# ScalarE seeds two kept PSUM banks with the doubled residual for the plain down products of a macaron decoder

## The chip, the core and the metric

The kernel runs on one core of one Trainium2 chip. The metric is the device time of one execution in microseconds (us). TensorE (PE in the profile, PEld for its weight loads) multiplies, VectorE (DVE) and ScalarE (ACT) do the elementwise work, and SyncE (SP) issues the DMAs. Products are summed in PSUM banks, of which the program uses eight as single tiles of 128 x 512 fp32.

## What is computed

Two layers of a decoder over 512 tokens with 1024 features. Each layer is an FFN half-step, a mixer (gated linear attention in the first, stick-breaking attention in the second) and another FFN half-step; a last RMSNorm follows.

```python
def swiglu(h, w_gate, w_up, w_down):
    return (jax.nn.silu(h @ w_gate) * (h @ w_up)) @ w_down
...
x = x + 0.5 * swiglu(rmsnorm(x, ffn1_norm[i]), ffn1_w_gate[i], ffn1_w_up[i], ffn1_w_down[i])
...
x = x + 0.5 * swiglu(rmsnorm(x, ffn2_norm[i]), ffn2_w_gate[i], ffn2_w_up[i], ffn2_w_down[i])
```

D_FF is 2816, all data are fp32. The change touches the four FFN half-steps only, in the line `x + 0.5 * (...) @ w_down`.

## The kernel before

**Layout.** The residual x stays in SBUF for the whole program as eight tiles `xs[k]` of 128 features x 512 tokens. Weights come from HBM in entries of up to 1 MB.

**A product in three passes.** Each fp32 operand is split into a high half rounded to the matmul's reduced format and a low remainder. For weights, ACT casts the high half (`wh`, L138) and DVE subtracts to get the low one (`wl`, L139); for activations the same is done in `cut` (L806 and L807). A product is then three matmuls, high by high, low by high and high by low (`mm3`, L82, through `mm`, L79; the profile shows these under L80).

**The feed.** The program is a list of entries (`Feed`, `Entry`): a load, a split and a body with the products. A started entry splits up to two entries after it ahead of time, and loads further. Bodies are generators; within an FFN they run one after another. Each engine works its own instruction list in order, and the order of a list comes from a scheduler that places instructions of the five engines by their dependences.

**PSUM banks.** `psum()` hands out one whole bank a call. Without a tag it takes the next letter of `order`, "aazzztto", and so goes through 8 banks in turn: two of tag a, three z, two t, one o. A bank can be written again when the reader of its last tile is done.

**An FFN phase** (class `FFN`, L605, run four times) splits the 11 column chunks of the gate and up weights in the groups `((0, 2), (2, 4), (4, 6), (6, 8), (8, 9), (9, 11))`. For the first chunks, gate and up tiles are plain products (`feat`); for the later ones they go through `seven()`, a Strassen-like scheme of seven half products in place of eight. A `seven` takes the banks `ps_w`, `ps_q` and `ps_z`. Its first product goes to `ps_w`; ACT copies it to `ps_z` (L736), onto which later products add without a fresh start; ACT copies further halves to SBUF (L739, L742, L754), DVE adds (L755, L759), and the gate is a Silu on ACT (L719) for the gate weights or a multiplication by it on DVE (L722) for the up weights. The last gate of an up `seven` reads `ps_w`, which frees it.

**Down.** A group's down products follow while the next group's gate and up run. Groups 1 and 3 use `seven_down` (L353), which opens two `ps_w` banks, copies them to two `ps_z` banks on ACT (L402), opens one `ps_q` (products L384) and adds to x on DVE (L390). Groups 0, 2 and 4 use `down` (L310): groups 0 and 2 have 4 entries of two output tiles, each tile 4 x 3 matmuls of 512 columns; group 4 has 2 entries of four output tiles with 2 x 3 matmuls each. The first two entries of group 0 run just ahead of group 1, and the first of them is given `late=1`: its two tiles are summed over three of four parts first, and then both are finished. After a tile's last product DVE adds half of it to x (L339). Group 5's entries also go through `down`, but with `nxt` set, which starts the next norm with each finished tile; in the last FFN `back_tok` and `to_tokens` do this part instead. The first FFN of the second layer follows the last FFN of the first layer at once.

**Where the FFN phases lie** in the trace: about 60 to 320, 607 to 862, 930 to 1190 and 1492 to 1747 us, called the first to the fourth FFN below. Outside of these lie the mixers, the norms and the transitions.

Of the kernel before, what the change touches and what calls it, by code (L numbers as in the profile page):

```python
# [14 lines left out]
AF = mybir.ActivationFunctionType  # L15
ALU = mybir.AluOpType
# [14 lines left out]
def turns(t):  # L31

    return t.rearrange("p (two n) -> p n two", two=2)


def flat(ps):

    return ps.rearrange("p (n two) -> p two n", two=2)


def pair(t):

    return t.rearrange("p (two n) -> p two n", two=2)
# [3 lines left out]
def decoder(ctx: ExitStack, tc: tile.TileContext, a: dict, out: bass.AP):  # L47
    nc = tc.nc
# [6 lines left out]
    sp = ctx.enter_context(tc.tile_pool(name="sp", bufs=1))  # L55
    pp = ctx.enter_context(tc.tile_pool(name="pp", bufs=1, space=PSUM))
    banks = {"a": 2, "z": 3, "t": 2, "o": 1}
    order = "aazzztto"
    turn_ = [0]

    def psum(name, tag=None):
        if tag is None:
            tag = order[turn_[0] % 8]
            turn_[0] += 1
        return pp.tile([P, T], F32, tag=tag, bufs=banks[tag], name=name)

# [9 lines left out]

    xs = [xp.tile([P, T], F32, name=f"x{k}") for k in range(KD)]

    def mm(ps, l, r, first, last):  # L79
        st["pe"] = nc.tensor.matmul(ps, l, r, start=first, stop=last).ins  # L80

    def mm3(ps, wh, wl, mh, ml, first, last):  # L82
        mm(ps, wh, turns(mh), first, False)
        mm(ps, wl, turns(mh), False, False)
        mm(ps, wh, turns(ml), False, last)

# [108 lines left out]
    def feat(ch, f, evac, tag=None, defer=None):  # L197


        def body(W):  # L200
            (wh, wl), = W
            ps = psum("ps_f", tag)
            for part in (range(u, u + KD // 4) for u in range(0, KD, KD // 4)):
                for k in part:
                    mm3(ps, wh[:, k], wl[:, k], st["h"][k], st["l"][k], k == 0, k == KD - 1)
                if part[-1] == KD - 1:
                    if defer is None:
                        evac(ps)
                    else:
                        defer.append((evac, ps))  # L210
                yield

        feed.q.append(Entry([(ch, lambda t: t[:, :, f * P : (f + 1) * P], KD, P)], body))
        feed.q[-1].evac = evac
# [29 lines left out]
    def back(w, r0, nf, hs, scale, nxt, late=0, tags=(None,) * 8):  # L244


        for dh in range(2):
# [18 lines left out]
            def acc(m, dh=dh, accs=accs):  # L266
                if m == len(accs):
                    accs.append(psum("ps_b", tags[dh * 4 + m]))
                return accs[m]

            def prod(W, u, kk, m, f, acc=acc):
                wh, wl = W[u]
                s = slice(m * P, (m + 1) * P)
                mm3(acc(m), wh[:, kk, s], wl[:, kk, s], hs[f][0], hs[f][1], f == 0, f == nf - 1)
# [37 lines left out]
    def down(w, r0, nf, hs, part, nxt, late=0):  # L312


        nd = KD // nf
        src = w[r0 : r0 + nf * P, part * nd * P : (part + 1) * nd * P]
        ch = Chunk(src.rearrange("(f p) c -> p f c", p=P), nf, nd * P)
        ch.few = True

        def body(W):  # L320
            (wh, wl), = W
            acc = []

            def prod(m, fs):
                if m == len(acc):
                    acc.append(psum("ps_d"))
                s = slice(m * P, (m + 1) * P)
                for f in fs:
                    mm3(acc[m], wh[:, f, s], wl[:, f, s], hs[f][0], hs[f][1], f == 0, f == nf - 1)

            if late:
                for m in range(nd):
                    prod(m, range(nf - late))
            for m in range(nd):
                prod(m, range(nf - late if late else 0, nf))
                ps = acc[m]
                k = part * nd + m
                x = pair(xs[k])
                nc.vector.scalar_tensor_tensor(  # L339
                    out=x, in0=flat(ps), scalar=0.5, in1=x, op0=ALU.mult, op1=ALU.add  # L340
                )
                if nxt is not None:
                    nxt(k)
                yield

        feed.q.append(Entry([(ch, lambda t: t, nf, nd * P)], body))

    def seven_down(pool, w, r0, hs, part):
# [128 lines left out]
    st = {}  # L477
# [76 lines left out]
    def sums_wide(pool):  # L554

        ss = st["ss"]
        h = sp.tile([P, T], F32R, tag="sq", name="sh")
        nc.scalar.copy(h, ss)
        l = pool.tile([P, T], F32R, tag="t", name="sl")
        nc.vector.tensor_tensor(out=l, in0=ss, in1=h.bitcast(F32), op=ALU.subtract)  # L560
        st["wide"] = ps = psum("ps_R")
        mm(ps, ones_r, turns(h), True, False)
        mm(ps, ones_r, turns(l), False, True)

    def rstd_wide():

        ps = st["wide"]
        v = sp.tile([P, T], F32, tag="ss", name="v")
        nc.vector.tensor_scalar(
            out=pair(v), in0=flat(ps), scalar1=1.0 / D, scalar2=EPS, op0=ALU.mult, op1=ALU.add  # L570
        )
        y = st["R"] = sp.tile([P, T], F32, tag="sq", name="R")
        act(y, v, AF.Ln)
        act(y, y, AF.Exp, scale=-0.5)
        nc.scalar.activation(ps, y, AF.Square)
        nc.vector.scalar_tensor_tensor(out=v, in0=ps, scalar=-0.5, in1=v, op0=ALU.mult, op1=ALU.mult)
        nc.vector.scalar_tensor_tensor(out=y, in0=v, scalar=1.5, in1=y, op0=ALU.add, op1=ALU.mult)

    def two_halves(between=None):

        feed.finish()
        g = [feed.start(), feed.start()]
        for i in range(3):
            for x in g:
                next(x, None), next(x, None)
            if i == 0 and between is not None:
                between()

    def new_norm():
        st["h"], st["l"] = st["nh"], st["nl"]  # L590

    def flush(deferred):
        for evac, ps in deferred:
            evac(ps)
        deferred.clear()

    def exp_ln_tables(after):
        with tc.issue_after(after):
            st["tab"] = nc.scalar.preload_act_table_set("natural_log_exp_and_others").ins
# [7 lines left out]
    class FFN:  # L607
# [294 lines left out]
        def run(self, between=None):  # L902
            with tc.tile_pool(name="hp", bufs=8, reuse_waits="tile") as self.hp, tc.tile_pool(
                name="tp", bufs=5, reuse_waits="tile"
            ) as self.tp:
                st["few"] = self.hp
                new_norm()
                if st["ss"] is not None:
                    if self.after_ffn:
                        exp_ln_tables(st["closed"])  # L910
                    two_halves(lambda: sums_wide(self.tp))
                    rstd_wide()
                flush(self.defer)
                def spread(todo, n):
                    for i in range(n):
                        for piece in todo[i * len(todo) // n : (i + 1) * len(todo) // n]:
                            piece()
                        feed.entries(1)

                spread(self.normed_input(), self.NORMED - 2)  # L920
                self.normed = True
                st["h"], st["l"] = zip(*self.n)
                todo = self.sums()
                spread(todo[:5], self.sums_by - self.NORMED)
                feed.entries(1, True)
                for piece in todo[5:]:
                    piece()
                feed.entries(self.count - self.sums_by - 1, True)
                if between is not None:
                    with tc.issue_after(st["closed"]):  # L930
                        nc.scalar.preload_act_table_set("sqrt_and_others")
                    feed.q[feed.pos].split()
                    between(self.tp)
                feed.entries(self.total - self.count)


    class GLA:
# [968 lines left out]
```

## Time and profile before

| what | value |
| --- | --- |
| runs, us | 1781.41, 1781.2, 1780.84 (median 1781.2) |
| the profiled execution, us | 1780.26 |
| its span from first to last instruction, us | 1778.3 |
| granted TensorE clock, mean | 1.00 |
| DMA moved | 179.24 MB, mean 101 GB/s |

The profile is one execution. A group's row gives its busy time, the mean of one instruction in ns, and the idle time of its engine ahead of it with the releaser. A timeline row begins with start and duration in us and names line, operation and tiles (out<-in); "x2" joins two of a kind. In brackets stands the idle time before it and the instruction that ended it. PE's matmuls overlap: a row lasts longer than the distance to the next. A row of the chain of waits gives the start, the time spent and the engine, tile, line and count.

### The profile page before, as it was taken

The page shows a single profiled execution, that of the slowest core. Times are in us where ns is not written, and L with a number is a line of the kernel's source. Part 1 is how long each engine was busy: PE and PEld are TensorE (multiplying, and loading weights), DVE is VectorE, ACT ScalarE, POOL GpSimd, SP SyncE. Part 2 cuts the span into 40 slices and gives each one's busy share as a digit, 9 for nine tenths or more (in the row PEclk, how much of TensorE's full clock was granted, in tenths as well). Part 3 has the DMA queues.
Part 4 walks back from the last instruction along what each step waited for, and adds up shares of the span by engine and source line. Part 5 has one row for each costly group of instructions (what it writes and reads, how often), then busy time and mean ns, then how long its engine had stood idle before and what let it go on. Part 6 is the DMA issues. An engine that isn't in the chain of part 4 may idle for free.

```text
span 1778.3 us, 31182 instructions
## 1 busy us (share of the span) xinstructions
PE 1760.1 (99%) x12714; PEld 1631.7 (92%) x12714; DVE 1538.5 (87%) x2527; ACT 1050.5 (59%) x1830; POOL 9.8 (1%) x24
## 2 busy tenths in 40 slices
PE   9999999999999999999999999999999999999998
PEld 8999999889888899999889999999888888999997
DVE  8999798786878999889798988977898679998986
ACT  7556455554655556555555555655888755565554
POOL 0000000100000000000000000000000000000000
PEclk9999999999999999999999999999999999999999
DMA  5433334322122333333333333322212233333331
GB/s 167 142 115 112 107 96 132 93 71 72 49 95 95 104 110 119 107 107 108 109 93 119 96 119 103 124 84 83 83 48 72 71 95 119 110 105 111 105 126 52
DMA packets 178755, 179.24 MB, mean 101 GB/s; under 512 B 4082, under 2 KB 170276, under 8 KB 178612
## 3 DMA queue, kind: packets, MB, share of 16 engines
q1 hardware_dynamic: 177760, 175.91, 31.6%
q8 instruction: 99, 1.62, 0.4%
q0 software_dynamic: 608, 1.05, 0.2%
q14 instruction: 44, 0.36, 0.1%
q10 hardware_dynamic: 244, 0.29, 0.0%
HBM read 175.17 MB, written 2.10 MB: 100 GB/s over the span
## 4 chain that ended last, share of the span: by engine, by line
PE 64%; DVE 25%; ACT 7%; issue 3%; DMA 1%; SPq 0%; DVEq 0%; ACTq 0%
PE ps_w L709 14%; PE ps_d L80 12%; PE ps_f L80 8%; DVE wl L139 7%; PE ps_q L709 7%; PE ps_t L80 5%; PE ps_z L709 3%; PE ps_b L80 3%; ACT wh L138 3%; PE ps_w L384 2%; DVE x L390 2%; DVE ts L816 1%; PE ps_q L384 1%; PE ps_z L1394 1%; DVE xn L800 1%
## 5 line engine op out<-in xcount | busy, mean ns | idle before, releaser
L139 DVE TENSOR_TENSOR wl<-raw,wh 128x1024 fp32r<-128x1024 f32 x241 | 254.9, 1058 | 58.1 <-ACT wh L138 57.5
L138 ACT CAST wh<-raw 128x1024 fp32r<-128x1024 f32 x241 | 221.6, 920 | 72.4 <-PE ps_f L80 21.5
L139 DVE TENSOR_TENSOR wl<-s,wh 128x1024 fp32r<-128x1024 f32 x176 | 214.2, 1217 | 42.2 <-ACT wh L138 41.9
L138 ACT CAST wh<-s 128x1024 fp32r<-128x1024 f32 x176 | 184.2, 1047 | 102.9 <-DVE s L701 25.7
L709 PE MATMUL ps_w<-th,wh 128*128 128x256 f32 x864 | 239.8, 278 | 3.7 <-ACT ps_z L736 2.7
L709 PE MATMUL ps_w<-th,wl 128*128 128x256 f32 x864 | 237.6, 275 | 0.0
L709 PE MATMUL ps_w<-tl,wh 128*128 128x256 f32 x864 | 237.6, 275 | 0.0
L709 PEld LDWEIGHTS ps_w<-th,wh 128*128 128x128 f32 x864 | 165.8, 192 | 7.4 <-ACT ps_z L736 7.1
L80 PE MATMUL ps_f<-xh,wh 128*128 128x512 f32 x432 | 166.8, 387 | 0.9 <-DVE x L260 0.9
L709 PEld LDWEIGHTS ps_w<-tl,wh 128*128 128x128 f32 x864 | 165.9, 192 | 0.0
L709 PEld LDWEIGHTS ps_w<-th,wl 128*128 128x128 f32 x864 | 165.8, 192 | 0.0
L80 PE MATMUL ps_f<-xh,wl 128*128 128x512 f32 x432 | 164.2, 380 | 0.5 <-DVE wl L139 0.5
L80 PE MATMUL ps_f<-xl,wh 128*128 128x512 f32 x432 | 164.0, 380 | 0.0
L80 PE MATMUL ps_d<-hl,wh 128*128 128x512 f32 x416 | 158.0, 380 | 0.9 <-DVE hl L807 0.8
L80 PE MATMUL ps_d<-hh,wh 128*128 128x512 f32 x416 | 157.7, 379 | 0.2 <-ACT hh L806 0.2
L80 PE MATMUL ps_d<-hh,wl 128*128 128x512 f32 x416 | 157.7, 379 | 0.0
L138 ACT CAST wh<-rawd 128x1024 fp32r<-128x1024 f32 (+1 forms) x100 | 82.9, 845 | 60.1 <-PE ps_d L80 45.2
L139 DVE TENSOR_TENSOR wl<-rawd,wh 128x1024 fp32r<-128x1024 f32 (+1 forms) x100 | 95.7, 961 | 14.7 <-ACT wh L138 14.7
L80 PEld LDWEIGHTS ps_f<-xh,wh 128*128 128x128 f32 x432 | 81.7, 189 | 12.1 <-DVE x L260 1.3
L80 PEld LDWEIGHTS ps_f<-xl,wh 128*128 128x128 f32 x432 | 81.7, 189 | 11.5
L80 PEld LDWEIGHTS ps_f<-xh,wl 128*128 128x128 f32 x432 | 81.7, 189 | 11.1 <-DVE wl L139 0.9
L339 DVE SCALAR_TENSOR_TENSOR x<-ps_d,x 128x512 f32<-128x512 f32 x120 | 79.8, 682 | 13.8 <-PE ps_d L80 13.7
(352 smaller groups left out, 5247.9 us busy)
## 6 DMA issues: line engine op xcount, KB each, us to landing
raw<-in_ffn_w_gate_dram SPq DMA_DIRECT2D x43, 1024.0 KB, 5.4
raw<-in_ffn_w_up_dram SPq DMA_DIRECT2D x43, 1024.0 KB, 5.3
rawd<-in_ffn_w_down_dram SPq DMA_DIRECT2D x84, 512.0 KB, 3.6
raw<-in_gla_w_in_dram SPq DMA_DIRECT2D x12, 1024.0 KB, 5.3
raw<-in_sb_w_in_dram SPq DMA_DIRECT2D x16, 512.0 KB, 3.7
raw<-in_gla_w_out_dram SPq DMA_DIRECT2D x4, 1024.0 KB, 5.2
raw<-in_sb_w_in_dram SPq DMA_DIRECT2D x4, 1024.0 KB, 5.0
raw<-in_sb_w_out_dram SPq DMA_DIRECT2D x4, 1024.0 KB, 5.1
```

Source lines behind the costliest of these rows:

```text
L80: st["pe"] = nc.tensor.matmul(ps, l, r, start=first, stop=last).ins
L138: st["cut"] = nc.scalar.copy(h[:, k], part).ins
L139: nc.vector.tensor_tensor(out=l[:, k], in0=part, in1=h[:, k].bitcast(F32), op=ALU.subtract)
L339: nc.vector.scalar_tensor_tensor(out=x, in0=flat(ps), scalar=0.5, in1=x, op0=ALU.mult, op1=ALU.add)
L384: st["pe"] = nc.tensor.matmul(ps, l_, r_, start=first and c + n == 0, stop=c == 1 and n == 2, skip_group_check=True).ins
L390: nc.vector.scalar_tensor_tensor(out=x, in0=ps, scalar=0.5, in1=x, op0=ALU.mult, op1=ALU.add)
L709: st["pe"] = nc.tensor.matmul(o, l_, r_, start=first and j + n == 0, stop=j == 3 and n == 2, skip_group_check=True).ins
L800: nc.vector.scalar_tensor_tensor(out=t, in0=xs[k], scalar=g, in1=st["R"], op0=ALU.mult, op1=ALU.mult)
L816: nc.vector.tensor_tensor(out=o, in0=p, in1=q, op=ALU.subtract)
L1394: nc.tensor.matmul(o_, l_, r_, start=first, stop=last, skip_group_check=True)
```

## The change

In an FFN phase the turn of banks becomes "aazzzo", six banks, and the two of tag t are kept for `down`. In every plain `down` entry without `nxt` (groups 0, 2 and 4, ten entries in each FFN) the first two tiles go to these two banks. The first two such tiles of each FFN are summed and added as before. For each later one, ACT writes 2x into the bank (new line L329 of the changed kernel), all products add to it without a fresh start, and ACT writes half of the bank back to x (L349) in place of DVE's half-add (now L351). In the entries with four tiles (group 4) the third and fourth tile stay as they were. After the phase the turn of eight banks comes back. Products, their order and the DMAs stay the same.

```diff
@@ -55,12 +55,12 @@
     sp = ctx.enter_context(tc.tile_pool(name="sp", bufs=1))
     pp = ctx.enter_context(tc.tile_pool(name="pp", bufs=1, space=PSUM))
     banks = {"a": 2, "z": 3, "t": 2, "o": 1}
-    order = "aazzztto"
+    order = ["aazzztto"]
     turn_ = [0]
 
     def psum(name, tag=None):
         if tag is None:
-            tag = order[turn_[0] % 8]
+            tag = order[0][turn_[0] % len(order[0])]
             turn_[0] += 1
         return pp.tile([P, T], F32, tag=tag, bufs=banks[tag], name=name)
 
@@ -76,13 +76,13 @@
 
     xs = [xp.tile([P, T], F32, name=f"x{k}") for k in range(KD)]
 
-    def mm(ps, l, r, first, last):
-        st["pe"] = nc.tensor.matmul(ps, l, r, start=first, stop=last).ins
-
-    def mm3(ps, wh, wl, mh, ml, first, last):
-        mm(ps, wh, turns(mh), first, False)
-        mm(ps, wl, turns(mh), False, False)
-        mm(ps, wh, turns(ml), False, last)
+    def mm(ps, l, r, first, last, onto=False):
+        st["pe"] = nc.tensor.matmul(ps, l, r, start=first, stop=last, skip_group_check=onto).ins
+
+    def mm3(ps, wh, wl, mh, ml, first, last, onto=False):
+        mm(ps, wh, turns(mh), first, False, onto)
+        mm(ps, wl, turns(mh), False, False, onto)
+        mm(ps, wh, turns(ml), False, last, onto)
 
 
 
@@ -319,14 +319,23 @@
 
         def body(W):
             (wh, wl), = W
-            acc = []
+            acc, seeded = [], []
+            if nxt is None:
+                for m in range(2):
+                    acc.append(psum("ps_s", "t"))
+                    seeded.append(st["seeds"] > 1)
+                    st["seeds"] += 1
+                    if seeded[m]:
+                        nc.scalar.activation(flat(acc[m]), pair(xs[part * nd + m]), AF.Copy, scale=2.0)
 
             def prod(m, fs):
                 if m == len(acc):
                     acc.append(psum("ps_d"))
+                    seeded.append(False)
                 s = slice(m * P, (m + 1) * P)
                 for f in fs:
-                    mm3(acc[m], wh[:, f, s], wl[:, f, s], hs[f][0], hs[f][1], f == 0, f == nf - 1)
+                    first, last = f == 0 and not seeded[m], f == nf - 1
+                    mm3(acc[m], wh[:, f, s], wl[:, f, s], hs[f][0], hs[f][1], first, last, seeded[m])
 
             if late:
                 for m in range(nd):
@@ -336,9 +345,12 @@
                 ps = acc[m]
                 k = part * nd + m
                 x = pair(xs[k])
-                nc.vector.scalar_tensor_tensor(
-                    out=x, in0=flat(ps), scalar=0.5, in1=x, op0=ALU.mult, op1=ALU.add
-                )
+                if seeded[m]:
+                    nc.scalar.activation(x, flat(ps), AF.Copy, scale=0.5)
+                else:
+                    nc.vector.scalar_tensor_tensor(
+                        out=x, in0=flat(ps), scalar=0.5, in1=x, op0=ALU.mult, op1=ALU.add
+                    )
                 if nxt is not None:
                     nxt(k)
                 yield
@@ -904,6 +916,7 @@
                 name="tp", bufs=5, reuse_waits="tile"
             ) as self.tp:
                 st["few"] = self.hp
+                order[0], st["seeds"] = "aazzzo", 0
                 new_norm()
                 if st["ss"] is not None:
                     if self.after_ffn:
@@ -932,6 +945,7 @@
                     feed.q[feed.pos].split()
                     between(self.tp)
                 feed.entries(self.total - self.count)
+                order[0] = "aazzztto"
 
 
     class GLA:
```

## The prediction

> **What bounds the kernel now.** I read the page's busy times first, then its chain, then the stretches of the four FFN phases, since only those run under the change.
>
> ```profile
> span 1778.3 us, 31182 instructions
> PE 1760.1 (99%) x12714; PEld 1631.7 (92%) x12714; DVE 1538.5 (87%) x2527; ACT 1050.5 (59%) x1830; POOL 9.8 (1%) x24
> PE 64%; DVE 25%; ACT 7%; issue 3%; DMA 1%; SPq 0%; DVEq 0%; ACTq 0%
> ```
>
> PE works 99% of the span. The chain gives DVE 25%, but a chain follows the event that came last by the profile and can run along a DVE stretch while PE works too. So the stretches decide (span, then busy us and count of PE, PEld, DVE, ACT, POOL, clock, DMA share, GB/s):
>
> ```profile
> 60.00:320.00 260.00, 259.23 (x2084) 251.29 (x2083) 234.72 (x382) 145.00 (x255) 7.77 (x15) 1.00 0.36 112
> 930.00:1190.00 260.00, 258.28 (x2080) 250.81 (x2080) 233.89 (x380) 143.82 (x253) 0.53 (x1) 1.00 0.34 106
> ```
>
> PE lacks 0.8 of 260 us in the first FFN and 1.7 in the third, at full clock and a DMA share of 0.36. PE is the bound; DVE, at 90%, is close behind. The waits of the weight loads (total, times, longest) show what a faster DVE or ACT could give back:
>
> ```profile
> PEld ps_w L709 <- ACT ps_z L736: 7.1, 18, 1.4
> PEld ps_w L384 <- DVE x L390: 1.3, 6, 0.3
> ```
>
> That is 8.4 us in 24 waits. After a wait the next matmul also starts late: the one that waited lasts 0.38 instead of 0.28 (rows at 949.58 and 948.12 below), so 0.10 more each, 10.8 us in all. This is the ceiling for a gain.
>
> The steady pitch, from the chain: 24 down products in 5.18 us, that is 2.59 a tile, and 12 of the seven-product kind in 1.34.
>
> ```profile
> 93.30 5.18 PE ps_d L80 x24
> 98.48 1.34 PE ps_w L709 x12
> ```
>
> **Removed and added work.** The removed instruction is DVE's half-add; ACT's seed and writeback have no row of their own, so I take ACT's nearest ones into and out of a bank.
>
> ```profile
> L339 DVE SCALAR_TENSOR_TENSOR x<-ps_d,x 128x512 f32<-128x512 f32 x120 | 79.8, 682 | 13.8 <-PE ps_d L80 13.7
> L1584 ACT ACTIVATE ps_bt<-x 128x512 f32<-128x512 f32 x7 | 4.2, 602 | 7.9 <-DVE x L1574 7.9
> L1567 ACT COPY x<-ps_T 128x512 f32<-128x512 f32 x8 | 4.0, 624 | 0.3 <-PE ps_T L1562 0.3
> ```
>
> Each FFN has 10 plain entries with two such tiles, of which the first two are not seeded: 4 x 18 = 72. DVE loses 72 x 0.682 = 49 us (87% to about 83%), ACT gains 72 x (0.602 + 0.624) = 88 us (59% to about 64%). PE's products and SP's DMAs are the same in number and order. So nothing follows from busy time: only what makes PE wait, or stop waiting, counts.
>
> **Term 1, the first seeded pair of each FFN: +8.2.** The first entry fills the two kept banks unseeded, and DVE empties them with the old half-add. The second entry follows directly on PE. Before, it took two fresh banks; now its first product waits for that half-add and then for a seed. DVE reaches the half-add late, behind splits. Per FFN: PE's first product of the second entry, DVE's half-adds, and for two of them what stands ahead on DVE.
>
> ```profile
> 58.98 0.38 PE L80 MATMUL ps_d<-hh,wh 128*128 128x512 f32 x1
> 58.78 1.22 DVE L139 TENSOR_TENSOR wl<-raw,wh 128x1024 fp32r<-128x1024 f32 x1
> 59.91 1.28 DVE L339 SCALAR_TENSOR_TENSOR x<-ps_d,x 128x512 f32<-128x512 f32 x2
> 606.39 0.38 PE L80 MATMUL ps_d<-hh,wh 128*128 128x512 f32 x1
> 606.42 1.28 DVE L339 SCALAR_TENSOR_TENSOR x<-ps_d,x 128x512 f32<-128x512 f32 x2
> 930.99 0.38 PE L80 MATMUL ps_d<-hh,wh 128*128 128x512 f32 x1
> 931.03 1.28 DVE L807 TENSOR_TENSOR tl<-ts,th 128x512 fp32r<-128x512 f32 x2
> 932.24 0.68 DVE L339 SCALAR_TENSOR_TENSOR x<-ps_d,x 128x512 f32<-128x512 f32 x1
> 1491.40 0.38 PE L80 MATMUL ps_d<-hh,wh 128*128 128x512 f32 x1
> 1491.50 1.28 DVE L339 SCALAR_TENSOR_TENSOR x<-ps_d,x 128x512 f32<-128x512 f32 x2
> ```
>
> The first half-add of each pair ends 0.68 after it starts; a handover takes about 0.04 (a product chain ends at 99.82, ACT's copy starts at 99.86, below) and ACT to PE about 0.06 (a copy ends at 949.52, PE starts at 949.58, below); the seed takes 0.60. So PE starts 1.38 us after DVE's half-add does: 61.29, 607.80, 933.62, 1492.88, which is 2.3 + 1.4 + 2.6 + 1.5 = 7.8 us late, with 4 x 0.10 for the slow restart 8.2. The change leaves DVE's order ahead of these half-adds as it was and takes nothing off DVE there. The second seed is not late: its product comes a tile of 2.59 later. Bounds: 2.9 if DVE were on time and only the seed and the restart counted (4 x 0.72); 10.6 if each seed stood one more ACT operation of 0.6 back. I take the worked value. Behind the waiting seed ACT has the second seed, then the writeback, which waits for PE itself, and then a cast that waited 7.55 us for DVE:
>
> ```profile
> 65.49 1.07 ACT L138 CAST wh<-s 128x1024 fp32r<-128x1024 f32 x1 [7.55 <-DVE s L701]
> ```
>
> So in the first FFN nobody else is held up; the cast can slip with PE. Every later seed has time: its bank is written back after the entry before, and between the two stand products of a seven (the entry that ends at 98.48 is followed by one), several times the seed's 0.60, so it costs PE nothing while ACT is not behind.
>
> **Term 2, six banks in turn: +2.7, small reuses +0.4.** Under eight banks the product of `seven_down` that opens `ps_q` found a long free bank. Under six it gets the bank of the preceding seven's `ps_w`, which DVE's gate L722 frees. I compared each reuse six allocations back with the row that frees it; three come out late by more than the handover:
>
> ```profile
> 1121.63 0.28 PE L384 MATMUL ps_q<-hh,wh 128*128 128x256 f32 x1
> 1119.15 1.05 ACT L138 CAST wh<-s 128x1024 fp32r<-128x1024 f32 x1 [0.91 <-PE ps_q L709]
> 1120.72 1.22 DVE L139 TENSOR_TENSOR wl<-s,wh 128x1024 fp32r<-128x1024 f32 x1
> 1122.46 0.41 DVE L722 TENSOR_TENSOR o<-ps_w,o 128x256 f32<-128x256 f32 x1
> 680.22 0.28 PE L384 MATMUL ps_q<-hh,wh 128*128 128x256 f32 x1
> 681.03 0.42 DVE L722 TENSOR_TENSOR o<-ps_w,o 128x256 f32<-128x256 f32 x1
> 824.68 0.28 PE L384 MATMUL ps_q<-hh,wh 128*128 128x256 f32 x1
> 825.12 0.42 DVE L722 TENSOR_TENSOR o<-ps_w,o 128x256 f32<-128x256 f32 x1
> ```
>
> The gates end at 1122.87, 681.45 and 825.54: 1.24 + 1.23 + 0.86 = 3.3 us late, the upper end. With DVE relieved the split ahead could start when its cast ends (1119.15 + 1.05 + 0.04 = 1120.24 instead of 1120.72), so 0.48 comes off, 0.76 remains, and for three 2.3, the lower end. I take 2.4, nearer the relieved case because DVE does lose work, and 0.3 for restarts. Reuses that come out within a few tenths (copies into `ps_z`, the last transposes) I put at 0.4, between 0 and one more gate of 1.3.
>
> **Term 3, ACT's queue: +0.5.** A writeback waits at the head of ACT's queue for the end of its tile, and behind it stand a cast, a seed and the `ps_z` copy on which the next seven depends.
>
> ```profile
> 98.52 1.07 ACT L138 CAST wh<-rawd 128x1024 fp32r<-128x1024 f32 x1 [2.55 <-PE ps_d L80]
> 99.86 0.36 ACT L736 COPY ps_z<-ps_w 128x256 f32<-128x256 f32 x1 [0.26 <-PE ps_w L709]
> ```
>
> Here the down tile ends at 98.48. Writeback to 99.14, cast to 100.2, seed to 100.8, less some 0.09 of overlap at each boundary (the DVE rows at 58.78 and 59.91 overlap so), copy to about 100.95. PE needs it when the `ps_q` products end, 99.82 + 1.34 = 101.16. So it is hidden by 0.2. There are about a dozen such passages: nothing if each keeps its 0.2, 2.6 if each misses by 0.2. I take 0.5.
>
> **Term 4, waits that go: -4.4.** Three waits close behind the FFN starts come from ACT and DVE running late there; a PE set back by term 1 no longer meets them.
>
> ```profile
> 948.12 0.28 PE L709 MATMUL ps_q<-tl,wh 128*128 128x256 f32 x1
> 949.15 0.37 ACT L736 COPY ps_z<-ps_w 128x256 f32<-128x256 f32 x1
> 949.58 0.38 PE L709 MATMUL ps_w<-th,wh 128*128 128x256 f32 x1 [1.19 <-ACT ps_z L736]
> 76.95 0.38 PE L709 MATMUL ps_w<-th,wh 128*128 128x256 f32 x1 [0.16 <-ACT ps_z L736]
> 1499.68 0.38 PE L709 MATMUL ps_w<-th,wh 128*128 128x256 f32 x1 [0.26 <-ACT ps_z L736]
> ```
>
> The first is 949.58 - 948.12 less the pitch of 0.11, 1.35; the idle shown is 0.16 shorter, so the others are 0.32 and 0.42; with restarts 2.4. Of the other 8.4 of the ceiling I take a quarter, 2.0: DVE's lighter load brings the sums earlier, but the copy itself hangs on ACT, which gets more to do. Bounds 0 and 8.4.
>
> **Sum.** 8.2 + 2.7 + 0.4 + 0.5 - 4.4 = +7.4 on the profiled execution's 1780.26 (span 1778.3 and 2.0 around it): 1787.7. The median of the runs, 1781.2, lies 0.9 above that execution; between the two I say 1788.
>
> **The rivals.** Relief of DVE wins (faster): all 10.8 us of waits go, term 1 falls to its 2.9 and term 2 to 2.3 + 0.3, so 1780.3 - 10.8 + 2.9 + 2.6 = 1775. For it: DVE's 87% and 25% of the chain. Against it: 7.1 of the 8.4 us wait on an ACT copy, and term 1's half-adds are late in a stretch where nothing leaves DVE. It decides once the `ps_z` waits fall below about 1 us and the first seeds cost under 1 us each; chance 0.08. [...]
>
> No change: terms 1 to 3 come, but the set-back lets DVE and ACT catch up for a whole FFN and all waits go, 11.8 - 10.8 = +1, 1782. For it: the waits are short (7.1 in 18). Against: they recur through the FFN, far from its start. Chance 0.2.
>
> ACT becomes the bound: each of the dozen passages misses by a seed less its slack, 0.4, and 0.1 for the restart, 13 x 0.5 = 6.5 instead of 0.5, 1794. For it: ACT works in order and its queue now has waits on PE in it. Against: ACT at 64%. Chance 0.14.
>
> That the accumulation fails to take up the seed isn't among them: L736 already lets ACT fill a bank to which products add.
>
> **How the numbers follow.** Forecast 0.58, rivals 0.08, 0.2, 0.14. About 0.2% or 3.6 us can be told from no change: below 1777.6 is faster, above 1784.8 slower. The forecast's own range is 1783 to 1792. Faster 0.09, same 0.21 (the second rival and the forecast's low edge), slower 0.70. The range 1781 to 1795 leaves out the first rival and the ends.
>
> **What would show it.** The waits should list four on ACT's seeds, 1.3 to 2.6 us each, 7.8 together, and three of some 0.8 of `seven_down`'s `ps_q` on DVE's gate; `ps_z` waits should fall from 7.1 to 3 or 4. DVE near 1490 us busy, ACT near 1138. Wrong if the seeds wait under 1 us each, or if `ps_z` waits grow past 9.

## The result and the profile after

The changed kernel takes 1791.84 us (median of 6 runs, 1790.88 to 1794.13), the kernel before 1781.06 (6 runs, 1780.36 to 1781.55): 10.8 us or 0.6% slower, ratio 1.0061 (95% interval 1.005 to 1.0072). The profiled execution took 1791.22, its span is 1789.1. The page's span and busy times after:

```profile
span 1789.1 us, 31200 instructions
PE 1761.2 (98%) x12714; PEld 1632.6 (91%) x12714; DVE 1502.7 (84%) x2455; ACT 1124.2 (63%) x1974; POOL 9.8 (1%) x24
```

DVE lost 36 us and ACT gained 74, so work did move as planned (less than the forecast 49 and 88, since neighbouring instructions overlap: two half-adds in a row last 1.28 us and not 2 x 0.68); PE's busy time grew by 1 us while the span grew by 10.8. PE waits more. Its weight loads' waits after (total, times, longest):

```profile
PEld ps_s L80 <- ACT ps_s L329: 8.7, 4, 2.8
...
PEld ps_w L721 <- ACT ps_z L748: 3.2, 11, 0.4
PEld ps_q L396 <- DVE o L734: 2.7, 3, 0.9
PEld ps_w L721 <- ACT u L766: 2.0, 2, 1.0
...
PEld ps_q L721 <- DVE x L402: 1.3, 2, 0.6
...
PEld ps_w L396 <- ACT ps_z L414: 1.0, 2, 0.6
```

The old waits on the `ps_z` copy fell from 7.1 to 3.2 us. Five new kinds stand beside them, the first seeds far ahead. To see where each us arises I paired the 12714 weight loads of the two traces in order and noted every step of 0.15 us or more in the difference of their starts:

```
four first seeds                                   +8.6
matmuls at half clock behind the third of them     +1.4
seven_down's ps_q behind DVE's gate (3 places)     +3.0
a seven's ps_q behind DVE's add to x (2)           +1.4
a seven's ps_w behind ACT's copy into u (2)        +2.2
other new waits, half of it on a ps_z copy (14)    +3.9
waits of before that went (25)                     -8.8
outside the FFNs, and steps under 0.15             -0.9
sum                                               +10.8
```

The costliest place is the start of the third FFN. PE, DVE and ACT there, in the timeline after (start, duration, line, tiles; in brackets the idle time before and what ended it):

```profile
935.46 0.38 PE L80 MATMUL ps_s<-hl,wh 128*128 128x512 f32 x1
938.28 0.79 PE L80 MATMUL ps_s<-hh,wh 128*128 128x512 f32 x1 [2.44 <-ACT ps_s L329]
938.87 0.63 PE L80 MATMUL ps_s<-hh,wl 128*128 128x512 f32 x1
939.30 0.63 PE L80 MATMUL ps_s<-hl,wh 128*128 128x512 f32 x1
...
941.40 0.38 PE L80 MATMUL ps_s<-hh,wl 128*128 128x512 f32 x1
941.62 0.38 PE L80 MATMUL ps_s<-hl,wh 128*128 128x512 f32 x1
```

```profile
935.71 1.28 DVE L819 TENSOR_TENSOR tl<-ts,th 128x512 fp32r<-128x512 f32 x2
936.91 0.68 DVE L351 SCALAR_TENSOR_TENSOR x<-ps_s,x 128x512 f32<-128x512 f32 x1
```

```profile
937.63 0.60 ACT L329 ACTIVATE ps_s<-x 128x512 f32<-128x512 f32 x1 [3.97 <-DVE x L351]
```

The reader sees the whole chain: DVE is busy with remainders while PE stands, its half-add comes at 936.91, the seed at 937.63, and PE restarts at 938.28. Then something new: the next matmuls follow at 0.43 us instead of 0.22 until 941.40. The stretches of the same place name it (span, busy us and count of PE, PEld, DVE, ACT, POOL, then the granted clock):

```profile
938.00:940.00 2.00, 1.72 (x4) 1.44 (x5) 2.00 (x5) 1.32 (x3) 0.00 (x0) 0.50 0.02 4
940.00:941.50 1.50, 1.50 (x5) 1.15 (x5) 1.50 (x2) 0.45 (x1) 0.00 (x0) 0.55 0.80 211
941.50:943.00 1.50, 1.50 (x9) 1.31 (x8) 1.50 (x4) 0.26 (x1) 0.00 (x0) 1.00 1.09 388
```

The clock is at half for 3.41 us, from 937.95 to 941.36 in the trace's record of the clock. Seven matmuls lose 0.2 us each, 1.4 together.

ACT's list also changed. Before, the copy into u stood ahead of a cast; after, the cast stands ahead, and it waits for a sum on DVE. ACT before, then ACT after, at the same place of the first FFN:

```profile
90.71 0.37 ACT L754 COPY u<-ps_w 128x256 f32<-128x256 f32 x1 [1.01 <-PE ps_w L709]
91.40 1.07 ACT L138 CAST wh<-s 128x1024 fp32r<-128x1024 f32 x1 [0.32 <-DVE s L695]
```

```profile
93.10 1.04 ACT L138 CAST wh<-s 128x1024 fp32r<-128x1024 f32 x1 [1.71 <-DVE s L707]
94.05 0.36 ACT L766 COPY u<-ps_w 128x256 f32<-128x256 f32 x1
```

The copy's source was ready in the 1.71 us in which ACT waited; PE's next product into `ps_w` waits for the copy.

### The profile page after: what moved, and what is told of

Read it like the earlier page. It is cut to its first block, busy times and chain, and to the rows that moved or that the text cites. A ratio compares the mean times of both kernels' runs of the same rounds, so it can differ in the third digit from the quotient of the medians.

```text
span 1789.1 us, 31200 instructions
## 1 busy us (share of the span) xinstructions
PE 1761.2 (98%) x12714; PEld 1632.6 (91%) x12714; DVE 1502.7 (84%) x2455; ACT 1124.2 (63%) x1974; POOL 9.8 (1%) x24
## 4 chain that ended last, share of the span: by engine, by line
PE 69%; DVE 23%; ACT 5%; issue 3%; DMA 1%; DVEq 0%; ACTq 0%; SPq 0%
PE ps_w L721 16%; PE ps_q L721 8%; PE ps_f L80 8%; PE ps_s L80 7%; DVE wl L139 6%; PE ps_t L80 5%; PE ps_z L721 4%; PE ps_d L80 4%; PE ps_w L396 4%; PE ps_b L80 3%; PE ps_q L396 2%; ACT wh L138 2%; DVE hl L819 1%; DVE nl L819 1%; DVE ts L828 1%
## 5 line engine op out<-in xcount | busy, mean ns | idle before, releaser
L80 PE MATMUL ps_s<-hh,wh 128*128 128x512 f32 x288 | 110.5, 384 | 7.4 <-ACT ps_s L329 7.1
L80 PE MATMUL ps_s<-hl,wh 128*128 128x512 f32 x288 | 109.9, 382 | 0.8 <-DVE hl L819 0.8
L80 PE MATMUL ps_s<-hh,wl 128*128 128x512 f32 x288 | 109.7, 381 | 0.0
L80 PEld LDWEIGHTS ps_f<-xl,wh 128*128 128x128 f32 x432 | 81.7, 189 | 11.4
L80 PEld LDWEIGHTS ps_f<-xh,wh 128*128 128x128 f32 x432 | 81.7, 189 | 10.8
L721 PE MATMUL ps_q<-th,wh 128*128 128x256 f32 x288 | 79.4, 276 | 0.9 <-DVE x L402 0.9
```

The lines of the kernel that those rows point to most:

```text
L721: st["pe"] = nc.tensor.matmul(o, l_, r_, start=first and j + n == 0, stop=j == 3 and n == 2, skip_group_check=True).ins
```

## The experiments

Each ran on one chip beside runs of the kernel before, whose medians were 1780.47, 1781.0 and 1781.08 us in the three groups. A difference below is to the median of its own group.

**The second entry in turn.** The wait on a first seed is taken away by leaving each FFN's second plain entry out of the kept banks.

```diff
             if nxt is None:
+                st["plain"] += 1
+            if nxt is None and st["plain"] != 2:
                 for m in range(2):
...
-                order[0], st["seeds"] = "aazzzo", 0
+                order[0], st["seeds"], st["plain"] = "aazzzo", 0, 0
```

> The second plain down entry of each FFN takes two banks of the six in turn and DVE's half-add; from the third entry on all is as in the changed kernel (64 seeds instead of 72). Theory (the first seeded pair is the main loss): the four waits on the seeds, 8.7 us in the trace, go, and with them the half-clock stretch behind the longest (eight matmuls 0.21 late each, 1.6 us), so about 1791.8 - 10.3 = 1781.5, clock 1.000. Rival (ACT's longer queue is the loss): ACT keeps 128 of its 144 added operations, so the time stays above 1788. Rival (six banks are the loss): two more tiles go through the turn of six, the waits move there, above 1786.

Measured 1784.66 us, +4.2 (ratio 1.0025, 1.0016 to 1.0034), 7.2 below the changed kernel's 1791.84 (6.6 by the differences to the two groups' own runs of the kernel before). No wait on a seed is left, and no half clock at the FFN starts (mean granted clock 0.999 against the changed kernel's 0.998). The theory's 1781.5 is missed by 3.2: the rest of the 10.3 came back elsewhere, which is what the rival on the banks said, though its price, above 1786, was too high:

```profile
PEld ps_w L723 <- ACT ps_z L750: 5.2, 13, 1.4
PEld ps_q L398 <- DVE o L736: 4.5, 5, 0.9
...
PEld ps_q L723 <- DVE x L404: 1.9, 3, 0.6
```

Five late gates instead of three and three late adds instead of two: +2.4. And without the set-back at the start of the third FFN the old wait of 1.4 us on the `ps_z` copy is there again. ACT's queue, with 128 of its 144 new operations, is not the main loss.

**Six banks alone.** The kernel before, with only the turn shortened.

```diff
-    order = "aazzztto"
+    order = ["aazzztto"]
...
+                order[0] = "aazzzo"
                 new_norm()
...
+                order[0] = "aazzztto"
```

> The kernel before with the turn of six banks in the FFNs and nothing else: no kept banks, no seeds, all half-adds on DVE, ten more tiles in each FFN's turn of six. Theory: the waits of seven_down's ps_q on DVE's gate (2.7 us in the changed kernel) and of a seven's ps_q on DVE's half-add (1.3) come, and a cast now stands ahead of the copy into u in ACT's list as in the changed kernel (2.0), so 4 to 7 us over before, 1785 to 1788; DVE isn't relieved here. Rival (banks don't matter, ACT's added work does): 1781 to 1782. Rival (six banks are the main loss): 1790 or more.

Measured 1791.88 us, +11.4 (1.0063, 1.0049 to 1.0076), beyond the expected 4 to 7 and as the second rival had it: two banks fewer cost as much as the whole change, without a single seed. The two totals are made up differently, though: here the twenty tiles of each FFN that the change gives to the kept banks go through the turn of six too (twenty, where the expectation says ten), and no product waits for a kept bank.

```profile
PEld ps_q L384 <- DVE o L722: 7.4, 5, 1.6
...
PEld ps_w L709 <- ACT ps_z L736: 4.2, 9, 1.4
PEld ps_w L709 <- ACT u L754: 3.0, 3, 1.0
PEld ps_q L709 <- DVE x L390: 2.5, 4, 0.6
...
PEld ps_w L384 <- ACT ps_z L402: 1.6, 3, 0.6
```

All new kinds of wait of the changed kernel but the seeds are here, the one on the copy into u too. So that order of ACT's list, with the cast at 91.73 and the copy at 92.68 in this run, comes with the shorter turn and not with seeds. The gate waits are longer than in the changed kernel (1.6 against 0.9 at most), because the gate stands behind one more item on a DVE that isn't relieved.

**Seeds in the turn of eight.**

```diff
-                    acc.append(psum("ps_s", "t"))
+                    acc.append(psum("ps_s"))
...
-                order[0], st["seeds"] = "aazzzo", 0
+                order[0], st["seeds"] = "aazzztto", 0
```

> The seeded tiles take ordinary banks of the turn of eight; the count of seeds and writebacks is that of the changed kernel (72 of each). [...] Theory (seeds cost only where a bank is free late): a bank of the turn of eight is free many products ahead, the first seeds wait for no half-add, ps_q finds its bank free; what is left is DVE's relief, some 4 to 6 us of old waits, so 1775 to 1778. Rival (ACT's queue is the loss): above 1785. Rival (no relief is to be had, the old waits hang on ACT): 1780 to 1783.

Measured 1778.15 us, -2.3 (0.9989, 0.998 to 0.9998), at the upper edge of the theory's 1775 to 1778. The output is off by a relative error of 1.01, so it is a time and no replacement. Its busy times, and the longest row of its waits in the FFNs; no wait on a seed or of a `ps_q` stands in the list:

```profile
PE 1759.2 (99%) x12714; PEld 1631.4 (92%) x12714; DVE 1499.9 (84%) x2455; ACT 1122.1 (63%) x1974; POOL 9.8 (1%) x24
```

```profile
PEld ps_w L721 <- ACT ps_z L748: 6.2, 16, 0.9
...
PEld ps_w L396 <- DVE x L402: 0.6, 3, 0.2
```

The same 144 operations on ACT, the same relief of DVE, all eight banks: a small gain, since 6.2 us of waits on the `ps_z` copy stay. ACT's copy into u is ahead of the cast again (90.92 and 91.61). ACT's longer queue isn't a loss on its own.

**The first seed twice.** The expectation speaks of the second seed of the pair; the edit doubles the first one, so the wait itself grows, and the ranges of the expectation don't apply.

```diff
-                        nc.scalar.activation(flat(acc[m]), pair(xs[part * nd + m]), AF.Copy, scale=2.0)
+                        for _ in range(2 if st["seeds"] == 3 else 1):
+                            nc.scalar.activation(flat(acc[m]), pair(xs[part * nd + m]), AF.Copy, scale=2.0)
```

> The changed kernel with the second seed of each FFN's first seeded pair written twice. Theory: the second seed has a tile of 2.59 us to hide in, so a second write of 0.6 is hidden in the first, second and fourth FFN; in the third the second seed ended at 940.46, at the edge, so 0 to 0.7 us: 1791 to 1793. Rival (ACT's queue is the loss): each write counts, 4 x 0.6 = 2.4, 1794 or more.

Measured 1798.2 us (4 runs, 1797.19 to 1801.8), 6.4 above the changed kernel, where four more seeds of 0.6 are 2.4. The seed waits grew by 2.6, as they should:

```profile
PEld ps_s L80 <- ACT ps_s L330: 11.3, 4, 3.5
```

Most of the rest is clock. In the profiled execution, 6.0 slower than that of the changed kernel, the pairing of weight loads puts 2.5 us on the four seeds and 3.0 on matmuls at half pitch in the first and fourth FFN; the last 0.5 is spread. Stretches that follow the wait in the first, second, third and fourth FFN:

```profile
61.90:66.00 4.10, 4.07 (x11) 3.36 (x12) 4.10 (x8) 0.50 (x1) 0.00 (x0) 0.58 0.01 2
...
612.00:616.00 4.00, 3.77 (x17) 3.32 (x18) 4.00 (x8) 1.51 (x4) 0.00 (x0) 1.00 0.00 0
...
941.00:945.00 4.00, 3.64 (x11) 3.03 (x12) 4.00 (x7) 1.86 (x3) 0.00 (x0) 0.69 0.62 204
...
1506.00:1510.00 4.00, 3.78 (x11) 3.13 (x12) 4.00 (x7) 1.73 (x3) 0.00 (x0) 0.60 0.19 45
```

Three of the four FFN starts now run at half clock for 3.4 us (0.58, 0.69 and 0.60 in the mean of these rows, 1.00 in the second), against one in the changed kernel: 2.6 us more of waits on the seeds came with 6.0 us more of time.

**The kept banks unseeded.** The first two tiles open the kept banks afresh, and DVE adds.

```diff
-                    seeded.append(st["seeds"] > 1)
+                    seeded.append(False)
```

> The changed kernel's banks, but no tile is seeded: the first two tiles of each plain entry go to the kept banks, open them afresh, and DVE adds half as before. Theory: at the four FFN starts PE waits for DVE's half-add alone, 8.7 less 4 x 0.62 = 6.2 us; no wait is over 2.2 us, so no half clock (1.6); DVE's relief is lost, which I put at 3 us by the six-bank run (its gate waits 1.6 instead of 0.9 at the longest): 1791.8 - 2.5 - 1.6 + 3 = 1790 to 1791. Rival (the relief is worth nothing, ACT's queue costs): 1786 to 1788.

Measured 1791.22 us, +10.2 (1.0056, 1.0043 to 1.007); the profiled execution, without a stretch at half clock in the FFNs (mean granted clock 0.999), took 1789.34. In the changed kernel's trace a start 2.5 late had gone on at full clock and one 2.8 late had not; that a wait of up to 2.2 leaves the clock full was the author's estimate, and the next run has a start at half clock behind 1.31 us of idle.

```profile
PEld ps_s L80 <- DVE x L351: 6.2, 4, 2.2
PEld ps_q L396 <- DVE o L734: 4.1, 3, 1.6
...
PEld ps_w L396 <- ACT ps_z L414: 2.8, 6, 0.6
PEld ps_w L721 <- ACT ps_z L748: 2.4, 7, 0.4
PEld ps_w L721 <- ACT u L766: 2.0, 2, 1.0
```

The first waits come out at the expected 6.2 and 2.2: the kept banks make PE wait for DVE's half-add, and the seed adds its 0.6 to it. The three gates that cost 2.7 in the changed kernel cost 4.1 here, and `seven_down`'s `ps_z` copies 2.8 instead of 1.0: this is where the relief of DVE shows. Two more readings matter. The waits on the copy into u are all here although ACT got no new operation (1051.3 us busy). And the old `ps_z` waits fell to 2.4 although DVE isn't relieved (1540.4 us busy): in the pairing with the kernel before, 8.9 us of old waits go at 25 places, against 8.8 at 25 in the changed kernel. So their fall doesn't need DVE's lighter load; a PE set back by the new waits, which no longer meets them, fits both runs.

**DVE writes back.**

```diff
-                    nc.scalar.activation(x, flat(ps), AF.Copy, scale=0.5)
+                    nc.vector.tensor_scalar(out=x, in0=flat(ps), scalar1=0.5, scalar2=None, op0=ALU.mult)
```

> The changed kernel with the writeback of the seeded tiles on DVE (half of the bank to x) in place of ACT: 72 operations go from ACT's queue to DVE's. Theory: the first seeds wait as before (8.7 us), DVE's relief is lost and ACT's shorter queue gives nothing: 1793 to 1796. Rival (writebacks at the head of ACT's queue are a loss of their own): 1790 or less.

Measured 1795.95 us, +15.0 (1.0085, 1.0072 to 1.0099): as expected, 4 above the changed kernel. The profiled execution took 1799.17, with three FFN starts at half clock where the changed kernel has one (mean granted clock 0.996 against 0.998). The seed waits are the same, the gates are back at 1.6:

```profile
PEld ps_s L80 <- ACT ps_s L329: 8.7, 4, 2.8
...
PEld ps_q L396 <- DVE o L734: 4.1, 3, 1.6
```

**The same in the turn of eight,** to price the relief where no bank is missing (the edit of the run with seeds in the turn of eight, and the one above: DVE writes the half back, and ACT has the seeds alone).

> [...] Theory (the gain of the seeds in the turn of eight is DVE's relief): the gain goes, 1780 to 1783. Rival (the gain comes from the seeds or from the order of the instructions): 1777 to 1779.

Measured 1784.22 us, +3.1 (1.0017, 1.0008 to 1.0026), 1.2 above the theory's range; its output is off by the same 1.01. Against the run with ACT's writeback (-2.3) taking 72 operations off DVE is worth 5.4 us here, though ACT gets them. Seeds without relief cost 3.1. In the pairing with the kernel before, 4.4 us of old waits go with ACT's writeback and 0.5 here. Some 3.5 of the 5.4 show as longer waits on the `ps_z` copy (8.3 against 6.2 us) and on DVE's add to x (2.0 against 0.6):

```profile
PEld ps_w L721 <- ACT ps_z L748: 8.3, 19, 1.4
...
PEld ps_w L396 <- DVE x L402: 2.0, 10, 0.3
```

**One kept bank, seven in turn.**

```diff
-                for m in range(2):
-                    acc.append(psum("ps_s", "t"))
-                    seeded.append(st["seeds"] > 1)
+                st["plain"] += 1
+            if nxt is None and st["plain"] != 2:
+                for m in range(1):
+                    acc.append(psum("ps_s", "o"))
+                    seeded.append(st["seeds"] > 0)
...
-                order[0], st["seeds"] = "aazzzo", 0
+                order[0], st["seeds"], st["plain"] = "aazzztt", 0, 0
```

> One kept bank and seven in turn: the first tile of each plain entry is seeded into the kept bank, the second is an ordinary one, and the second entry of each FFN is wholly ordinary, so that no product follows the first unseeded tile at once (32 seeds). Theory: no wait on a first seed; the late reuses of six banks have one allocation more and mostly go; a half of DVE's relief: 1779 to 1782. Rival (each bank taken from the turn costs alike, 11.4 us for two): 1785 to 1787.

Measured 1784.72 us, +3.7 (1.0021, 1.0012 to 1.0029): the theory's 1779 to 1782 missed, and just under the rival's 1785 to 1787. Seven banks still bring `seven_down`'s `ps_q` behind a gate, in five places:

```profile
PEld ps_w L723 <- ACT ps_z L750: 7.0, 19, 1.4
...
PEld ps_q L398 <- DVE o L736: 4.7, 5, 1.0
...
PEld ps_w L723 <- ACT u L768: 2.0, 2, 1.0
```

**GpSimd adds instead of a seed.** Eight banks; ACT copies half of the bank to one SBUF tile, GpSimd adds it to x.

```diff
+                if nxt is None and m < 2:
+                    t = st["few"].tile([P, T], F32, tag="half", bufs=1, name="half")
+                    nc.scalar.activation(pair(t), flat(ps), AF.Copy, scale=0.5)
+                    nc.gpsimd.tensor_tensor(out=xs[k], in0=t, in1=xs[k], op=ALU.add)
...
```

> The kernel before, eight banks in turn, no seeds: for the first two tiles of each plain entry ACT copies half of the bank to SBUF and GpSimd adds it to x, so DVE loses 80 half-adds. Theory (what is to be gained is DVE's relief, and a seed isn't needed for it): as with seeds in the turn of eight, 1777 to 1780. Rival (GpSimd's adds are slow or hold up DVE): above 1783; ACT's extra work alone: 1781 to 1783.

Measured 1846.43 us, +65 (1.0363, 1.0349 to 1.0377). GpSimd's adds take 2.29 us in the mean, 1.28 in the median and 6.73 at most, and PE waits up to 4.6 us for a `ps_z` copy:

```profile
L342 POOL TENSOR_TENSOR x<-half,x 128x512 f32<-128x512 f32 x80 | 183.3, 2291 | 1463.6 <-ACT half L341 1161.4 <-DVE tl L812 302.3
```

```profile
PEld ps_w L714 <- ACT ps_z L741: 56.5, 28, 4.6
```

The half tile has one buffer, so ACT's next half, and all behind it, must wait for GpSimd's add (33 times, 119.8 us of ACT's idle time). The mean granted clock is 0.989 in this run. How much of the 65 us is the buffer, how much GpSimd's speed and how much the clock was not taken apart; the run says nothing on the relief.

**Seeds by the state of the bank.** In the turn of eight, the seeds chosen by the width over which a bank was last opened.

```diff
-                    acc.append(psum("ps_s", "t"))
-                    seeded.append(st["seeds"] > 1)
+                    acc.append(psum("ps_s", None, "all"))
+                    seeded.append(st["was"])
...
+                    s = slice(0, P if seeded[m] == "low" else 2 * P)
+                    nc.scalar.activation(x[:, :, s], flat(ps)[:, :, s], AF.Copy, scale=0.5)
+                if seeded[m] == "low":
+                    x, f = (t[:, :, P :] for t in (x, flat(ps)))
```

> Eight banks in turn, no kept banks. A tile of the first two of each plain entry is seeded by its bank's last opening: where the bank was opened over its full width (23 tiles of 80) as in the changed kernel; where it was opened over its lower half (52), the lower half adds to the seed and ACT writes it back, and DVE half-adds the upper half of 128x256; 5 are unseeded. DVE loses 23 x 0.68 + 52 x (0.68 - 0.42) = 29 us instead of 49. Theory (eight banks and DVE's relief): a gain of 1 to 2 us, 1779 to 1780. Rival (ACT's extra work shows once DVE's relief is smaller): 1781 to 1783.

Measured 1780.16 us, -0.9 (0.9996, 0.9987 to 1.0005): no change that the runs can tell, between the theory and the kernel before. Its output is off too, by a relative error of 0.50, so it is a time and no replacement, and it does not show that its seeds are all taken up.

## Why the prediction came out as it did

The forecast was 1788, the range 1781 to 1795; 1791.84 lies within it, 3.8 above the forecast. The direction and the first term were right, the price of six banks and the waits that go were mis-sized in opposite directions, and one cost was missing. In the pairing's terms the forecast +7.4 becomes +10.8 by 0.4 for term 1, 1.4 for the clock, 6.9 for terms 2 and 3, -4.4 for term 4 and -0.9 outside of the terms. That the time fell so near the forecast is partly luck.

**Term 1, right.** Predicted 2.3, 1.4, 2.6, 1.5 and a restart of 0.1 each, 8.2 together; in the trace 2.5, 1.6, 2.8 and 1.7, 8.6. The chain is the one worked out: DVE's late half-add, then the seed. The unseeded kept banks confirm the split (6.2 without the seeds), and leaving the second entry out takes the waits away.

**Missing: the clock.** The sum took a wait of PE at its length. The third FFN's start paid 1.4 us more because the clock fell to half. It is shown by the granted clock in the rows (0.50 and 0.55 from 938.00 to 941.50), and by the doubled seed, which put three starts at half clock. Which starts are hit isn't set by the wait alone: with the same seed waits (8.7 us in four), the run in which DVE writes back had three.

**Term 2, the gates: right in kind and place.** Three late gates were predicted at 680, 824 and 1121 us for 2.7; they came at these places for 3.0. The reuse of a seven's `ps_q` behind DVE's add (1.4) went into "small reuses, 0.4", which was too little. It came 0.7 late at two places that the comparison of reuses did not list.

**Terms 2 and 3: the shorter turn cost 10.5 and not 3.6.** "There are about a dozen such passages: nothing if each keeps its 0.2" looked for the cost of ACT's queue at passages after a down entry. The trace has 6.1 us of further new waits. The copy into u, 1.1 late twice, lost its place in ACT's list to a cast that waits for DVE; 3.9 more came in fourteen waits of 0.15 to 0.7, half of it on `ps_z` copies, in `seven_down` too. But this isn't ACT's queue. The unseeded kept banks, without a new operation on ACT, show the waits on u unchanged and 4.9 us of the others, and with seeds in the turn of eight the copy keeps its place. So the step that failed is the price of six banks: the comparison looked at when a bank comes free in the lists as they were, and the lists themselves changed.

**Term 4, wrong in size the other way: -4.4 against -8.8.** The three waits behind the FFN starts went as worked out (-1.46, -0.43 and -0.53 in the trace against 1.45, 0.42 and 0.52). Of the rest I took a quarter, for DVE's lighter load; nearly all went, and not for that reason, since 8.9 went without any relief. That the set-back of PE takes them all is likely and was not tested by itself. In the turn of eight 4.4 us of old waits go with the relief and 0.5 without it, and it is worth 5.4 us in all.

**The rivals.** "Relief of DVE wins" holds once the banks are left alone: with seeds in the turn of eight the time falls by 2.3, not to its 1775, because 6.2 us of `ps_z` waits stay. Taking 72 operations off DVE was worth 5.4 us between the two runs in the turn of eight, though ACT got them; in the change this gain was less than what the kept banks cost. "ACT becomes the bound" gave 1794, nearer to the measured time than the forecast, but it falls as a cause: the same ACT work in the turn of eight is faster than before, and the kept banks cost 10.2 without it. "No change" falls with the clear +10.8.

What was not tried: holding ACT's copy into u ahead of the cast with the banks as in the changed kernel, so its 2.2 us are read from the trace and not from an edit.

## What to carry to other kernels

Banks taken out of a rotation are paid wherever the next tenant comes one lap sooner, and a late reader on a busy engine sets the price: two banks cost 11.4 us here in the kernel without seeds. A seed in a bank needs that bank emptied and refilled before the first product, so never let the product follow the bank's last tenant at once: here it cost 8.7 us of waits at four places. Price a shorter turn with the order of the lists that come out of it, and not on the old lists alone: here a cast slipped ahead of a copy and PE waited 2.2 us. And don't book every old wait that goes as the gain of a relieved engine, since a set-back from elsewhere can hide it too.

## What the runs showed of the hardware

In the changed kernel's trace the granted clock fell to half at one of the four FFN starts, for 3.41 us from 937.95 on. The wait there left PE 2.44 us of idle time before 938.28, and matmuls of 512 columns then came every 0.43 us instead of 0.22 until 941.40. In the same trace the first FFN's wait, with 2.14 us of idle, was followed by matmuls at the full pitch, with a granted clock of 1.00 from 61.40 to 65.00:

```profile
61.40 0.48 PE L80 MATMUL ps_s<-hh,wh 128*128 128x512 f32 x1 [2.14 <-ACT ps_s L329]
61.72 0.38 PE L80 MATMUL ps_s<-hh,wl 128*128 128x512 f32 x1
61.94 0.38 PE L80 MATMUL ps_s<-hl,wh 128*128 128x512 f32 x1
```

Lengthening the waits by some 0.6 each (11.3 us in four, in place of 8.7) brought the half clock at three places of four. The fourth FFN's wait left 1.31 us of idle both in the changed kernel and in the run in which DVE writes back. The first went on at full clock (1.00 from 1502.00 to 1506.00), the second at half:

```profile
1501.96 0.48 PE L80 MATMUL ps_s<-hh,wh 128*128 128x512 f32 x1 [1.31 <-ACT ps_s L329]
```

```profile
1507.80 0.80 PE L80 MATMUL ps_s<-hh,wh 128*128 128x512 f32 x1 [1.31 <-ACT ps_s L329]
```

In the second of these runs the clock is at half from 63.64 to 67.05, from 944.28 to 947.69 and from 1507.47 to 1510.89, 3.41 or 3.42 us each time. So the idle time of one wait doesn't tell by itself whether the half clock comes with it; what else does was not shown.

In the run in which GpSimd adds, half of its 80 adds of 128x512 fp32 took 1.28 us or less, where DVE's half-add takes 0.68. The mean is 2.29, since some last up to 6.73 us; what held those up was not looked into.
